# Two sums of weights of a seven-product unit made by accumulating DMAs, one over a tile that ScalarE negates

## The chip, the core and the metric

The kernel runs on one core of a Trainium2 chip. The metric is the time of one execution in microseconds (us); the profile's own span is a little shorter. Engines are named as the profile names them: PE (TensorE's matmuls), PEld (its weight loads), DVE (VectorE), ACT (ScalarE), POOL (GpSimd) and SP (SyncE, which here issues the loads).

## What is computed

A decoder trunk of two layers on 256 positions of width 2048, in float32. The part that the change touches is the second half of a layer, the feed-forward block with a hidden width of 5632:

```python
h = rms_norm(x, ffn_norm[l])
x = x + (jax.nn.silu(h @ w_gate[l]) * (h @ w_up[l])) @ w_down[l]
```

The first half (a projection `w_in`, spatial gating and dilated attention, a projection `w_out`) is not touched.

## The kernel before

All matrix products run in a split form: an operand is cut into a high part, which ACT makes by a copy to a shorter float, and a low part, which DVE makes as operand minus high part. A product is then three matmuls (high by high, high by low, low by high). For weights `split_w` does this: `wh` is the high tile (ACT), `wl` the low tile (DVE), each 128x2048, for a slab of 1 MB that SP has loaded as a tile `raw`.

The feed-forward block goes in units (function `unit`). A unit has to multiply a two by two block matrix of activations by a two by two block matrix of weights, B11, B12, B21 and B22, each a 1 MB quarter. It does so with seven products in place of eight, the Winograd form of Strassen's scheme. The seven run on PE in the order r1, r5, r6, r2, r7, r3, r4, each of 12 matmuls of 512 columns, and add into four PSUM banks named C, CX, CZ and CY. Each has a preparation p1 to p7 that splits its weights:

- `early` makes e = B12 - B11 in a new tile, and over B12's tile B22 - B12, the sum that p7 splits;
- p1 splits B11, and then makes over its tile the sum that p6 splits;
- p5 splits e, p6 splits that sum;
- p2 makes over B11's tile the sum that p4 splits (B21 minus it), and then splits B21;
- p7 splits B12's tile, p3 splits B22, p4 splits B11's tile.

So before the change a unit has four sums of tiles on DVE: e, the one over B12's tile, and two over B11's tile. Behind the seven products stand four plain slabs of weights, 24 matmuls each.

A layer has 17 units: eleven for gate and up (in chunks of four, four and three), and after each chunk two for down. The two down units of a layer's third chunk have quarters of half the size (128x1024). Both layers make 34.

The order of the instructions is written out by the program itself: a list of items (one a product or a plain slab) is run in order; `prep_more` prepares an item as soon as the slots of a ring (UNIT_RING = 6, most items take two) allow it, about three items ahead of PE. `early` is called one item before p1 (`early_at`; five items before for a layer's first unit). Side work (copies out of PSUM, transposes, gating) is put between by `run_jobs`, when a planner's account of the engines' queues (class `Queues`, with costs `act_cost` and `dve_cost`) says that its input is ready. Every engine runs its own instructions in that order and waits on semaphores. ACT, DVE and POOL are called through a wrapper, so that their instructions have line L90 in the profile; matmuls have L836 (`mm3`), the loads L796 (`dma_one`), transposes L253.

Of the kernel before, what the change touches and what calls it, by code (L numbers as in the profile page):

```python
# [11 lines left out]
ACTF = mybir.ActivationFunctionType  # L12
ALU = mybir.AluOpType
# [10 lines left out]
W = 512  # L24
# [8 lines left out]
KC = 4  # L33
HK = 2
S_GU = 4
FORMS = ("11", "22", "S1", "S3", "S2", "12", "S4")

SLOTS = 22
PLAIN_RAW, PLAIN_RING = 3, 4
# [102 lines left out]
def trunk_kernel(ctx: ExitStack, tc: tile.TileContext, aps: dict):  # L142
    nc = tc.nc
    PSUM = bass.MemoryType.PSUM
    q = Queues()
    act = Engine(q, nc.scalar, "act", act_cost)
    dve = Engine(q, nc.vector, "dve", dve_cost)
# [16 lines left out]
    def slot(shape, dtype, name):  # L164

        return gen.tile(list(shape), dtype, tag="g", name=name)
# [65 lines left out]
    def drain(ready):  # L232
        stuck = 0
        while not ready():
            assert stuck < 2000, "operand is never made"
            stuck += 1
            q.pe += 100
            run_jobs(1000)
# [344 lines left out]
    class Forms:  # L583
# [5 lines left out]
        def at(self, f):  # L589
            h = self.halves[FORMS.index(f)]  # L590
            return h[:, 0, :self.s, :], h[:, 1, :self.s, :]
# [27 lines left out]
    def make_forms(F, xg):  # L619

        def quarter(t, h):
            return xg[:, h, :F.s, t * P:(t + 1) * P]
        a11, a12, a21, a22 = quarter(0, 0), quarter(0, 1), quarter(1, 0), quarter(1, 1)

        def split(f, src):
            hi, lo = F.at(f)
            act.activation(out=hi, in_=src, func=ACTF.Copy)
            dve.tensor_tensor(out=lo, in0=src, in1=hi.bitcast(F32), op=ALU.subtract)
            F.ready.add(f)
        split("11", a11)  # L630
        split("22", a22)
        dve.tensor_tensor(out=a22, in0=a21, in1=a22, op=ALU.add)
        dve.tensor_tensor(out=a21, in0=a11, in1=a21, op=ALU.subtract)
        yield
        split("S1", a22)
        split("12", a12)
        dve.tensor_tensor(out=a11, in0=a22, in1=a11, op=ALU.subtract)
        dve.tensor_tensor(out=a12, in0=a12, in1=a11, op=ALU.subtract)
        yield
        split("S2", a11)  # L640
        split("S3", a21)
        split("S4", a12)

# [50 lines left out]
    class Chunk:  # L694
# [32 lines left out]
        def form(self, f, k):  # L727
            drain(lambda: self.F is not None)
            return self.F.get(f, k)
# [61 lines left out]
    def dma_one(r):  # L791
        n = sum(src.shape[1] for src in r.srcs)
        r.tile = slot([P, n, W], F32, "raw")
        k = 0
        for src in r.srcs:
            nc.sync.dma_start(out=r.tile[:, k:k + src.shape[1], :], in_=src)  # L796
            k += src.shape[1]
        live[0] += 1
# [6 lines left out]
    def need(r):  # L805
        while r.tile is None:
            dma_one(raws[n_raw[0]])
            n_raw[0] += 1
        return r.tile

    def split_w(src, parts=1):

        n = src.shape[1]
        if 2 * n <= 4:
            both = slot([P, 2, n, W], F32R, "w")
            wh, wl = both[:, 0], both[:, 1]
        else:
            wh, wl = slot([P, n, W], F32R, "wh"), slot([P, n, W], F32R, "wl")
        saved, q.chain = q.chain, q.pe
        for k in range(parts):  # L820
            sl = slice(k * n // parts, (k + 1) * n // parts)
            act.activation(out=wh[:, sl, :], in_=src[:, sl, :], func=ACTF.Copy)
            dve.tensor_tensor(
                out=wl[:, sl, :], in0=src[:, sl, :], in1=wh[:, sl, :].bitcast(F32), op=ALU.subtract)
        q.chain = saved
        return wh, wl

    def w_sum(out, in0, in1, op):
        saved, q.chain = q.chain, q.pe
        dve.tensor_tensor(out=out, in0=in0, in1=in1, op=op)  # L830
        q.chain = saved

    def mm3(out, x, wh, wl, start, stop):
        hi, lo = x
        for n, (a, b) in enumerate(((hi, wh), (hi, wl), (lo, wh))):
            nc.tensor.matmul(  # L836
                out=out, lhsT=a, rhs=b, start=start and n == 0, stop=stop and n == 2,
                skip_group_check=True)
# [32 lines left out]
    def unit(s, quarter, plains, form, done, lead=1):  # L871

        bank = {}
        b11, b12, b22, b21 = (Raw([quarter(*kn)], UNIT_RAW) for kn in ((0, 0), (0, 1), (1, 1), (1, 0)))
        raws.extend((b11, b12, b22, b21))
        U = {}

        def new_bank(name):  # L880
            drain(lambda: mm_lease.free)
            mm_lease.free.pop(0)
            bank[name] = mm_p.tile([P, W], F32, tag="mm", name="C" + name)

        def copy(out, in_):
            saved, q.chain = q.chain, q.pe
            act.activation(out=out, in_=in_, func=ACTF.Copy)
            q.chain = saved

        def early():  # L890
            x11, x12, x22 = need(b11), need(b12), need(b22)
            U["e"] = slot([P, s, W], F32, "e")
            live[0] += 1
            w_sum(U["e"], x12, x11, ALU.subtract)
            w_sum(x12, x22, x12, ALU.subtract)

        def p1(it, parts=1):
            it.w = split_w(b11.tile)
            w_sum(b11.tile, b12.tile, b11.tile, ALU.add)

        def p5(it, parts=1):
            it.w = split_w(U["e"])
            live[0] -= 1

        def p6(it, parts=1):
            it.w = split_w(b11.tile)

        def p2(it, parts=1):
            w_sum(b11.tile, need(b21), b11.tile, ALU.subtract)
            it.w = split_w(b21.tile)  # L910
            live[0] -= 1

        def p7(it, parts=1):
            it.w = split_w(b12.tile)
            live[0] -= 1

        def p3(it, parts=1):
            it.w = split_w(b22.tile)
            live[0] -= 1

        def p4(it, parts=1):
            it.w = split_w(b11.tile)
            live[0] -= 1

        def product(it, f, name, start):
            wh, wl = it.w
            for k in range(s):
                x = form(f, k)
                mm3(bank[name], x, wh[:, k, :], wl[:, k, :], start and k == 0, k == s - 1)
                q.pe += 3 * MM_NS  # L930
                run_jobs()

        def r1(it):
            new_bank("1")
            product(it, "11", "1", True)
            new_bank("X")
            copy(bank["X"], bank["1"])

        def r5(it):
            new_bank("Z")  # L940
            product(it, "S1", "Z", True)
            U["s5"], U["s3"] = (tmp.tile([P, W], F32, tag="u", name=n) for n in ("s5", "s3"))
            copy(U["s5"], bank["Z"])

        def r6(it):
            product(it, "S2", "X", False)
            new_bank("Y")
            copy(bank["Y"], bank["X"])

        def r2(it):  # L950
            product(it, "12", "1", False)

        def r7(it):
            product(it, "S3", "X", False)
            copy(U["s3"], bank["X"])

        def r3(it):
            product(it, "S4", "Y", False)
            w_sum(bank["Z"], bank["Z"], U["s3"], ALU.add)

        def r4(it):
            product(it, "22", "X", False)
            w_sum(bank["Y"], bank["Y"], U["s5"], ALU.add)

        for p, r in ((p1, r1), (p5, r5), (p6, r6), (p2, r2), (p7, r7), (p3, r3), (p4, r4)):
            items.append(Item(1 if s <= 2 else 2, UNIT_RING, p, r))
        early_at[len(items) - 7 - lead] = early

        names = {(0, 0): "1", (1, 0): "Y", (0, 1): "X", (1, 1): "Z"}
        for i, (n, srcs, ops) in enumerate(plains):  # L970
            r = Raw(srcs, UNIT_RAW)
            raws.append(r)

            def prep(it, parts=1, r=r):
                it.w = split_w(need(r))
                live[0] -= 1

            def run(it, i=i, n=n, ops=ops):
                wh, wl = it.w
                for t in range(NT):  # L980
                    for k, op in enumerate(ops):
                        mm3(bank[names[n, t]], op(t), wh[:, k, :], wl[:, k, :], False, k == len(ops) - 1)
                        q.pe += 3 * MM_NS
                        run_jobs()
                    if i >= len(plains) - 2:
                        add(done(n, t, bank[names[n, t]]), FFN_LIMIT)
            items.append(Item(2, UNIT_RING, prep, run))
# [238 lines left out]
```

## Time and profile before

| what | before |
|---|---|
| median of 3 runs | 2301.93 us (2301.18 to 2302.52) |
| profiled execution | 2301.2 us |
| its span | 2299.0 us |
| PE busy | 2261.3 us (98%) |
| DVE busy | 1834.0 us (80%) |
| ACT busy | 1325.0 us (58%) |
| POOL busy | 52.4 us (2%) |
| DMA queue of SP | 438.69 MB, 53.0% of 16 engines' span |

The span is the time between the first and the last profiled instruction; the profiled execution's own time is 2.2 us more. A busy share is that of the engine's instructions, and matmuls overlap, so that 98% of PE doesn't say that no matmul waited. DMAs issued by POOL don't occur in this kernel.

### The profile page before, as it was taken

The page shows a single profiled execution, that of the slowest core. Times are in us where ns is not written, and L with a number is a line of the kernel's source. Part 1 is how long each engine was busy: PE and PEld are TensorE (multiplying, and loading weights), DVE is VectorE, ACT ScalarE, POOL GpSimd, SP SyncE. Part 2 cuts the span into 40 slices and gives each one's busy share as a digit, 9 for nine tenths or more (in the row PEclk, how much of TensorE's full clock was granted, in tenths as well). Part 3 has the DMA queues.
Part 4 walks back from the last instruction along what each step waited for, and adds up shares of the span by engine and source line. Part 5 has one row for each costly group of instructions (what it writes and reads, how often), then busy time and mean ns, then how long its engine had stood idle before and what let it go on. Part 6 is the DMA issues. An engine that isn't in the chain of part 4 may idle for free.

```text
span 2299.0 us, 25930 instructions
## 1 busy us (share of the span) xinstructions
PE 2261.3 (98%) x10249; PEld 1864.1 (81%) x10249; DVE 1834.0 (80%) x1721; ACT 1325.0 (58%) x1590; POOL 52.4 (2%) x36
## 2 busy tenths in 40 slices
PE   9999999999999999999999999999999999999999
PEld 7888888878788878888788888887787888788887
DVE  6666766889999898998765666768899998989986
ACT  6455565565664665656555555646656556556563
POOL 0100000000000000000000001000000000000000
PEclk9999999999999999999999999999999999999999
DMA  9554455454465644745545444554545556447453
GB/s 361 176 183 165 165 175 204 174 198 165 183 237 183 224 179 159 264 181 201 183 174 193 164 165 165 183 212 173 183 165 198 223 186 235 165 165 274 165 201 110
DMA packets 66937, 440.33 MB, mean 192 GB/s; under 512 B 8064, under 2 KB 8576, under 8 KB 16768
## 3 DMA queue, kind: packets, MB, share of 16 engines
q1 hardware_dynamic: 66816, 438.69, 53.0%
q8 instruction: 80, 1.31, 0.2%
q14 instruction: 41, 0.34, 0.0%
HBM read 436.56 MB, written 2.10 MB: 191 GB/s over the span
## 4 chain that ended last, share of the span: by engine, by line
PE 77%; DVE 13%; issue 5%; ACT 3%; DMA 2%; SPq 0%; DVEq 0%; ACTq 0%
PE Z L836 30%; PE CX L836 15%; PE C L836 12%; PE CY L836 9%; PE CZ L836 8%; DVE wl L90 6%; ACT wh L90 2%; DVE raw L90 1%; PE sc L462 1%; DVE w L90 1%; DVE e L90 1%; PE hTp L253 1%; DMA gn<-in_k_norm 1%; PE qkp L253 1%; DVE hF L90 1%
## 5 line engine op out<-in xcount | busy, mean ns | idle before, releaser
L90 DVE TENSOR_TENSOR wl<-raw,wh 128x2048 fp32r<-128x2048 f32 x316 | 717.3, 2287 | 139.3 <-ACT wh L90 136.5
L90 ACT ACTIVATE wh<-raw 128x2048 fp32r<-128x2048 f32 x316 | 597.0, 1912 | 165.3 <-PE CX L836 56.3
L836 PE MATMUL Z<-w,xT 128*128 128x512 f32 x2688 | 641.5, 395 | 1.8 <-DVE xT L90 1.0
L836 PEld LDWEIGHTS Z<-w,xT 128*128 128x128 f32 x2688 | 499.2, 188 | 106.2 <-DVE w L90 1.6
L90 DVE TENSOR_TENSOR w<-raw,w 128x1024 fp32r<-128x1024 f32 (+1 forms) x313 | 376.9, 1217 | 214.8 <-ACT w L90 209.7
L90 ACT ACTIVATE w<-raw 128x1024 fp32r<-128x1024 f32 (+1 forms) x313 | 315.5, 1049 | 28.2 <-DMA raw<-in_w_in 9.1
L90 DVE TENSOR_TENSOR raw<-raw 128x2048 f32<-128x2048 f32 (+1 forms) x102 | 220.7, 2164 | 2.5
L836 PE MATMUL CX<-wh,fF 128*128 128x512 f32 x528 | 175.5, 391 | 1.5 <-ACT s L90 1.5
L836 PE MATMUL C<-wh,fF 128*128 128x512 f32 x352 | 118.7, 393 | 0.0
L836 PEld LDWEIGHTS CX<-wh,fF 128*128 128x128 f32 x528 | 99.1, 188 | 23.5 <-ACT s L90 2.4
L836 PE MATMUL CY<-wh,fT 128*128 128x512 f32 x352 | 115.9, 390 | 0.4
L836 PE MATMUL C<-wh,fT 128*128 128x512 f32 x352 | 115.6, 389 | 0.0
L836 PE MATMUL CZ<-wh,fT 128*128 128x512 f32 x352 | 115.5, 389 | 0.0
L836 PE MATMUL CX<-wh,fT 128*128 128x512 f32 x352 | 115.5, 389 | 0.0
L836 PE MATMUL CX<-wl,fF 128*128 128x512 f32 x264 | 102.7, 389 | 0.0
L90 ACT ACTIVATE CX<-C 128x512 f32<-128x512 f32 x34 | 19.8, 582 | 125.0 <-PE C L836 125.0
L836 PE MATMUL Z<-w,bT 128*128 128x512 f32 x384 | 89.9, 391 | 0.0
L836 PE MATMUL Z<-w,aT 128*128 128x512 f32 x384 | 89.1, 390 | 0.0
L836 PEld LDWEIGHTS Z<-w,aT 128*128 128x128 f32 x384 | 71.8, 188 | 14.8
L836 PEld LDWEIGHTS Z<-w,bT 128*128 128x128 f32 x384 | 71.8, 188 | 14.7
L836 PE MATMUL CY<-wh,fF 128*128 128x512 f32 x240 | 78.9, 390 | 0.0
L836 PEld LDWEIGHTS CY<-wh,fT 128*128 128x128 f32 x352 | 66.1, 188 | 15.6 <-issue 2.0
(191 smaller groups left out, 3445.0 us busy)
## 6 DMA issues: line engine op xcount, KB each, us to landing
raw<-in_w_in SPq DMA_DIRECT2D x109, 1024.0 KB, 4.8
raw<-in_w_gate SPq DMA_DIRECT2D x88, 1024.0 KB, 4.8
raw<-in_w_up SPq DMA_DIRECT2D x88, 1024.0 KB, 4.9
raw<-in_w_down SPq DMA_DIRECT2D x72, 1024.0 KB, 4.9
raw<-in_w_out SPq DMA_DIRECT2D x32, 1024.0 KB, 4.8
raw<-in_w_down SPq DMA_DIRECT2D x32, 512.0 KB, 4.6
raw<-in_w_in SPq DMA_DIRECT2D x5, 512.0 KB, 8.1
xstage<-in_xT SPq DMA_DIRECT2D x8, 256.0 KB, 7.4
```

The costliest lines, as they stand in the source:

```text
L90: return f(**kw)
L253: nc.tensor.transpose(out=tp[:, i, t * P:(t + 1) * P], in_=src_of(t)[:, (c0 + i) * P:(c0 + i + 1) * P], identity=ident)
L462: nc.tensor.matmul(out=sc[:, g, :n], lhsT=L.kv[pair, g][:, h, t * P:(t + 1) * P], rhs=kT[:, h, :n], start=True, stop=True)
L836: nc.tensor.matmul(out=out, lhsT=a, rhs=b, start=start and n == 0, stop=stop and n == 2, skip_group_check=True)
```

## The change

The sum over B12's tile is no longer made on DVE. ACT negates the tile in place (a copy with scale -1), and a DMA issued by POOL then adds B22 to it, read a second time from DRAM. The sum that p4 splits is made in the same way: as soon as p6 has split B11's tile, a DMA issued by POOL adds B21 to it from DRAM; p2 then only splits B21. For the signs to fit, the sum that p6 splits is now made as e - B22, the negative of what it was, and so the form of the activations in that product is the negative of S2 (`make_forms`: a11 - a22 in place of a22 - a11, and an addition in place of a subtraction behind it). The activations' work keeps its count of instructions. Each accumulating DMA is cut into pieces by `max_dma_last_dim=2 * W`.

```diff
         def early():
             x11, x12, x22 = need(b11), need(b12), need(b22)
             U["e"] = slot([P, s, W], F32, "e")
             live[0] += 1
             w_sum(U["e"], x12, x11, ALU.subtract)
-            w_sum(x12, x22, x12, ALU.subtract)
+            saved, q.chain = q.chain, q.pe
+            act.activation(out=x12, in_=x12, func=ACTF.Copy, scale=-1.0)
+            q.chain = saved
+            nc.gpsimd.dma_start(
+                out=x12, in_=quarter(1, 1), accum_op=ALU.add, max_dma_last_dim=2 * W)
 
         def p1(it, parts=1):
             it.w = split_w(b11.tile)
-            w_sum(b11.tile, b12.tile, b11.tile, ALU.add)
+            w_sum(b11.tile, U["e"], b22.tile, ALU.subtract)
...
         def p6(it, parts=1):
             it.w = split_w(b11.tile)
+            nc.gpsimd.dma_start(
+                out=b11.tile, in_=quarter(1, 0), accum_op=ALU.add, max_dma_last_dim=2 * W)
 
         def p2(it, parts=1):
-            w_sum(b11.tile, need(b21), b11.tile, ALU.subtract)
-            it.w = split_w(b21.tile)
+            it.w = split_w(need(b21))
             live[0] -= 1
...
         def r6(it):
-            product(it, "S2", "X", False)
+            product(it, "-S2", "X", False)
```

The planner counts the new costs, so side work moves as well. The place shown is the second down unit of a layer's first chunk. On DVE before, from e to p2's split (`raw_4748` is B11's tile, `raw_4778` B12's, `raw_4799` B22's, `raw_4818` B21's; `xs` are additions to the residual):

```order
L90 TENSOR_TENSOR e_4850<-raw_4778,raw_4748 128x2048
L90 TENSOR_TENSOR raw_4778<-raw_4799,raw_4778 128x2048
L90 TENSOR_TENSOR wl_4878<-raw_4748,wh_4877 128x2048
L90 TENSOR_TENSOR raw_4748<-raw_4778,raw_4748 128x2048
L90 TENSOR_TENSOR xs0_85<-C1_4667,xs0_85 128x512
L90 TENSOR_TENSOR wl_4908<-e_4850,wh_4907 128x2048
L90 TENSOR_TENSOR xs1_86<-CX_4681,xs1_86 128x512
L90 TENSOR_TENSOR xs0_85<-CY_4724,xs0_85 128x512
L90 TENSOR_TENSOR wl_4940<-raw_4748,wh_4939 128x2048
L90 TENSOR_TENSOR xs1_86<-CZ_4690,xs1_86 128x512
L90 TENSOR_TENSOR raw_4748<-raw_4818,raw_4748 128x2048
L90 TENSOR_TENSOR wl_4961<-raw_4818,wh_4960 128x2048
```

The same stretch of DVE now (`raw_4764` is B11's tile, `raw_4785` B12's, `raw_4804` B22's, `raw_4825` B21's):

```order
L90 TENSOR_TENSOR e_4855<-raw_4785,raw_4764 128x2048
L90 TENSOR_TENSOR wl_4884<-raw_4764,wh_4883 128x2048
L90 TENSOR_TENSOR raw_4764<-e_4855,raw_4804 128x2048
L90 TENSOR_TENSOR xs0_85<-C1_4673,xs0_85 128x512
L90 TENSOR_TENSOR wl_4914<-e_4855,wh_4913 128x2048
L90 TENSOR_TENSOR xs1_86<-CX_4687,xs1_86 128x512
L90 TENSOR_TENSOR xs0_85<-CY_4729,xs0_85 128x512
L90 TENSOR_TENSOR wl_4946<-raw_4764,wh_4945 128x2048
L90 TENSOR_TENSOR xs1_86<-CZ_4695,xs1_86 128x512
L90 TENSOR_TENSOR wl_4967<-raw_4825,wh_4966 128x2048
```

Two sums are gone, the one behind e and the one ahead of p2's split; the rest stands as it stood. On ACT before, in the same unit, from the split of the last plain slab ahead of the unit to p4's split:

```order
L90 ACTIVATE wh_4846<-raw_4730 128x2048
L90 ACTIVATE wh_4877<-raw_4748 128x2048
L90 ACTIVATE wh_4907<-e_4850 128x2048
L90 ACTIVATE wh_4939<-raw_4748 128x2048
L90 ACTIVATE CX_4957<-C1_4943 128x512
L90 ACTIVATE wh_4960<-raw_4818 128x2048
L90 ACTIVATE s5_4979<-CZ_4966 128x512
L90 ACTIVATE wh_4982<-raw_4778 128x2048
L90 ACTIVATE CY_5000<-CX_4957 128x512
L90 ACTIVATE wh_5002<-raw_4799 128x2048
L90 ACTIVATE wh_5020<-raw_4748 128x2048
```

And on ACT now:

```order
L90 ACTIVATE wh_4851<-raw_4735 128x2048
L90 ACTIVATE raw_4785<-raw_4785 128x2048
L90 ACTIVATE wh_4883<-raw_4764 128x2048
L90 ACTIVATE wh_4913<-e_4855 128x2048
L90 ACTIVATE wh_4945<-raw_4764 128x2048
L90 ACTIVATE CX_4964<-C1_4950 128x512
L90 ACTIVATE wh_4966<-raw_4825 128x2048
L90 ACTIVATE s5_4985<-CZ_4972 128x512
L90 ACTIVATE wh_4988<-raw_4785 128x2048
L90 ACTIVATE CY_5006<-CX_4964 128x512
L90 ACTIVATE wh_5008<-raw_4804 128x2048
L90 ACTIVATE wh_5026<-raw_4764 128x2048
```

The negation stands ahead of p1's split, which it was not behind before; the last row, p4's split of B11's tile, now waits for a DMA of POOL where it waited for DVE. POOL has no instruction in this unit before, and now the two DMAs.

## Rows read from the trace of the kernel before

**Rows 1.** The page's first part: busy time, share, instructions of each engine.

```profile
PE 2261.3 (98%) x10249; PEld 1864.1 (81%) x10249; DVE 1834.0 (80%) x1721; ACT 1325.0 (58%) x1590; POOL 52.4 (2%) x36
```

**Rows 2.** Busy time by stretch: first layer's feed-forward block, then second layer's first half.

```profile
core 0: us, PE busy (x) PEld busy (x) DVE busy (x) ACT busy (x) POOL busy (x), PEclk, DMA share, GB/s
400.00:1130.00 730.00, 712.76 (x3182) 585.31 (x3180) 643.18 (x416) 431.22 (x372) 0.69 (x1) 1.00 0.54 195
1130.00:1560.00 430.00, 429.75 (x2017) 358.51 (x2018) 281.15 (x452) 241.27 (x441) 24.88 (x14) 1.00 0.51 181
```

**Rows 3.** Waits of PE: who waited for whom, total us, times, longest us.

```profile
PE C L836 <- DVE wl L90: 12.7, 14, 1.2
PE CZ L836 <- DVE s L90: 5.4, 4, 1.4
```

**Rows 4.** Groups by shape: DVE's sums over a tile, ACT's split (busy us, mean ns).

```profile
L90 DVE TENSOR_TENSOR raw<-raw 128x2048 f32<-128x2048 f32 x90 | 206.0, 2289 | 2.1
L90 DVE TENSOR_TENSOR raw<-raw 128x1024 f32<-128x1024 f32 x12 | 14.7, 1225 | 0.4
L90 ACT ACTIVATE wh<-raw 128x2048 fp32r<-128x2048 f32 x316 | 597.0, 1912 | 165.3 <-PE CX L836 56.3 <-DVE wl L90 52.4 <-PE CZ L836 25.0
```

**Rows 5.** Timeline of the unit shown in order: DVE, ACT, PE (start us, us).

```profile
648.11 2.29 DVE L90 TENSOR_TENSOR wl<-raw,wh 128x2048 fp32r<-128x2048 f32 x1 [1.34 <-ACT wh L90]
650.44 2.29 DVE L90 TENSOR_TENSOR e<-raw 128x2048 f32<-128x2048 f32 x1
652.77 2.29 DVE L90 TENSOR_TENSOR raw<-raw 128x2048 f32<-128x2048 f32 x1
654.98 2.28 DVE L90 TENSOR_TENSOR wl<-raw,wh 128x2048 fp32r<-128x2048 f32 x1
...
660.11 2.28 DVE L90 TENSOR_TENSOR wl<-e,wh 128x2048 fp32r<-128x2048 f32 x1
...
664.38 2.29 DVE L90 TENSOR_TENSOR wl<-raw,wh 128x2048 fp32r<-128x2048 f32 x1 [0.79 <-ACT wh L90]
...
667.19 2.28 DVE L90 TENSOR_TENSOR raw<-raw 128x2048 f32<-128x2048 f32 x1
669.39 6.88 DVE L90 TENSOR_TENSOR wl<-raw,wh 128x2048 fp32r<-128x2048 f32 x3
...
662.42 1.92 ACT L90 ACTIVATE wh<-raw 128x2048 fp32r<-128x2048 f32 x1 [3.64 <-DVE wl L90]
...
668.42 1.91 ACT L90 ACTIVATE wh<-raw 128x2048 fp32r<-128x2048 f32 x1
...
674.56 1.92 ACT L90 ACTIVATE wh<-raw 128x2048 fp32r<-128x2048 f32 x1 [0.93 <-PE C L836]
...
671.73 0.50 PE L836 MATMUL C<-wl,hF 128*128 128x512 f32 x1 [0.90 <-DVE wl L90]
...
680.02 0.39 PE L836 MATMUL CX<-wl,hF 128*128 128x512 f32 x1
```

**Rows 6.** Timeline of PE in the chunk's last gate unit: the two matmuls that waited.

```profile
579.03 0.47 PE L836 MATMUL CZ<-wh,fF 128*128 128x512 f32 x1 [1.35 <-DVE s L90]
...
586.20 0.50 PE L836 MATMUL C<-wl,fF 128*128 128x512 f32 x1 [1.24 <-DVE wl L90]
```

**Rows 7.** Timeline of an ordinary gate unit: p6's low part (DVE), first matmuls of r4 (PE).

```profile
530.85 2.28 DVE L90 TENSOR_TENSOR wl<-raw,wh 128x2048 fp32r<-128x2048 f32 x1
...
550.18 0.39 PE L836 MATMUL CX<-wl,fF 128*128 128x512 f32 x1
```

**Rows 8.** Loads between 600 and 690 us: GB/s in 40 slices; tile raw's landings.

```profile
GB/s 269 197 0 7 0 0 29 350 87 0 135 331 69 335 291 401 382 379 131 350 55 328 84 0 0 0 0 0 266 200 95 393 339 200 422 393 411 441 426 149
...
DMA to landing us min/median/max: 4.7/4.9/8.0
```

**Rows 9.** Groups on POOL: its smallest frequent operations.

```profile
L90 POOL TENSOR_TENSOR qf<-rsq,mhalf 128x8 f32<-128x8 f32 x16 | 35.6, 2227 | 375.9 <-DVE rsq L90 375.9
L90 POOL TENSOR_TENSOR r<-rsq,mhalf 128x2 f32<-128x2 f32 x4 | 2.8, 698 | 925.3 <-DVE rsq L90 925.3
```

More of the change, by code (lines that the diff above doesn't have):

```diff
@@ L35 @@
 S_GU = 4
-FORMS = ("11", "22", "S1", "S3", "S2", "12", "S4")
+FORMS = ("11", "22", "S1", "S3", "-S2", "12", "S4")
 SLOTS = 22
@@ L636, in make_forms @@
         split("12", a12)
-        dve.tensor_tensor(out=a11, in0=a22, in1=a11, op=ALU.subtract)
-        dve.tensor_tensor(out=a12, in0=a12, in1=a11, op=ALU.subtract)
+        dve.tensor_tensor(out=a11, in0=a11, in1=a22, op=ALU.subtract)
+        dve.tensor_tensor(out=a12, in0=a12, in1=a11, op=ALU.add)
         yield
-        split("S2", a11)
+        split("-S2", a11)
         split("S3", a21)
```

## Prediction

> **What bounds the kernel now.** The page's first part comes first: PE is busy for 98% of the span [rows 1], so a saving on any other engine is worth only the waits of PE that it ends. The table by stretch tells where such waits can be. In the second layer's first half PE stands still for 430.00 - 429.75 = 0.25 us, in the first layer's feed-forward block for 730.00 - 712.76 = 17 us, with DVE busy for 643.18 of 730 us there [rows 2]. The units of the change lie in that block. The table of waits names the releasers: PE waited 14 times for DVE's low parts of weights in bank C, 12.7 us in all, and 4 times for DVE's reading of a bank that CZ needs, 5.4 us [rows 3]. What DVE's lateness costs is mostly in these 18.1 us; two such blocks of 17 us idle, 34 us or 1.5%, are the most that any change to DVE can give back, whatever it saves in DVE's own time.
>
> **What is removed.** Two sums a unit go from DVE, 30 units with full quarters and 4 with halves: 60 x 2.289 + 8 x 1.225 = 147 us of DVE work [rows 4]. Nearly all of it lay beside PE's work. What it is worth must be read where PE waits.
>
> The unit shown in order is the second down unit of a chunk [rows 5]. PE waits 0.90 us in r2 for the low part of B21, which p2's split makes. In front of that split DVE makes the sum for p4, and in front of all the sum for p7. The rest of the sum is what stands in their place. Its e starts when it did, since DVE waited for ACT just ahead of it (1.34 us, at 648.11), so nothing backs up into this unit.
>
> **What is added on ACT.** A negation of 34 tiles, taken at the price of a split of the same size, 1.91 us [rows 4]. It must wait for e, which reads the tile, and p1's split is queued behind it on ACT. In the unit: e ends at 652.73, the negation at 654.6, p1's high part at 656.6; DVE's p1 low part starts at 656.6 where it started at 654.98 [rows 5]. So one of the two sums taken from DVE is spent on waiting for ACT, and what follows is 1.6 us later than before, not 2.3 us earlier: p6's low part runs from 666.0 to 668.3 instead of 664.38 to 666.67. (p6's high part started when the low part of e was done, 662.4 [rows 5], and moves along.) The second sum is saved in full: p2's low part starts where the sum at 667.19 stood, plus 1.6, and ends at 668.8 + 2.3 = 671.1, against 669.39 + 2.29 = 671.7 before. **The wait of r2 shrinks by 0.6 us**, of 0.90.
>
> For the sum over all units: eight such down units at 0.6 give 4.8 us. The four last gate units of a chunk wait twice, 1.35 and 1.24 us [rows 6]; the second hangs on p2's low part behind a sum with a DVE that works without a break, and I take it as gone (5.0 us). The first hangs on a DVE queue that the negation holds up as well, and I take two thirds of 5.4, 3.6 us. The two waits of the 14 that are left give 1 us at most. Together 14 us. The ordinary gate units wait for nothing of DVE in these rows and give nothing. Forms of activations: the same count of instructions, no change.
>
> **What is added on POOL and the DMA engines.** Two transfers of 1 MB a unit, 60 MB and 4 more in halves. POOL is nearly empty in the block (0.69 us of 730 [rows 2]), so neither transfer queues there. Who waits for them is ACT, and behind a waiting ACT its copies out of PSUM and the next splits.
>
> The sum for p7 has time: ready for the DMA at 654.6, it is split at 668.42 [rows 5], 13.8 us later. The sum for p4 has not. Its DMA can start when p6's low part has been made, at 668.3 by the working above. r4 wants p4's low part at its second matmul, at 680.02 [rows 5], less the 0.6 gained, so 679.4. In front of that lie ACT's 1.92 and DVE's 2.29 us. So the tile must have landed by 679.4 - 4.2 = 675.2: **an allowance of 6.9 us**, in which p4's split can also slip from 674.56 without any cost. In an ordinary gate unit the same working gives much more: p6's low part ends at 533.1, r4's second matmul is at 550.18, less 4.2 that is 12.8 us [rows 7]. The tight units are the eight down units and, by the same crowded DVE queue, the four last gate units: twelve.
>
> How long does an accumulating DMA take? No row shows one. The nearest is a plain load of 1 MB issued by SP: 4.7 us when nothing else runs, up to 8.0 beside another one [rows 8]. The engines move up to 441 GB/s [rows 8], so 2.4 us of the 4.7 is movement. The low end is the plain load, 4.7 us. An accumulation has to read the tile that it writes, a second pass of up to 2.4 us. About half of the time another load is under way, and I add half of the 3.3 us that this costs at most, 1.6. For POOL's part in starting it, the nearest rows are its tiny operations, 0.7 to 2.2 us [rows 9]; I take the lower. That is 4.7 + 2.4 + 1.6 + 0.7 = **9.4 us**. The high end takes all of the 3.3 and the 2.2: 12.6 us.
>
> The Trainium skill, "DMA: Bandwidth & Descriptors" (Anatomy of one DMA, the GpSimd path), gives a DMA from POOL as 2.0 us plus its bytes at 436 GB/s, an estimate of 4.4 us for this tile; by that page alone nothing would be late and the sum would be 2287. "Collectives: The Full Stack" (The bandwidth ceiling) says that an add in the DMA engines reads two sources and halves the rate, which speaks against the change and would make it 6.8, by a hair in time. No run so far shows either.
>
> **The sum.** 9.4 us against an allowance of 6.9 makes r4 wait 2.5 us in twelve units: 30 us. Less the 14 us gained, +16. The profiled execution took 2301.2 us (2.2 over its span, 0.7 under the median), so **2317 us**. At the high end the wait is 5.7 x 12 = 68 us, less 14, and the time 2355; at the low end there is no wait and it is 2287, with all 18.1 us of waits gone 2283. The traffic itself, 64 MB over 438, some of it in two passes, fits: the queue is busy for about half of the block [rows 2], and loads have several us in hand.
>
> **Rivals.**
> In time: the accumulation lands in under 7.5 us, because the second read runs beside the write and loads don't collide. Then only the gain is left: 2301.2 - 14 = 2287, between 2282 and 2296. For it: the DMA engines are idle for 46% of the block [rows 2]; against it: bursts of loads in the very stretch in which it runs [rows 8]. It decides at about 8.1 us (1.2 us x 12 = 14).
>
> A draw: about 8.1 us, gain and waits cancel, 2301 +- 4.
>
> Much later: the transfer takes 15 us, because POOL writes its many small pieces (order shows the tile as eight pieces of 256 a partition) slowly. Then twelve units wait 8.1 us, the 18 ordinary gate units 2.2: 97 + 40 - 14 = +123, 2424. The place is the same, r4; it starts to be felt in gate units at 12.8 us.
>
> The change not doing what it says, a sum still on DVE, is excluded by the order of the instructions.
>
> **How the numbers follow.** Late in the tight units only: 0.50. Much later: 0.06. In time: 0.30. Draw: 0.14. A measurement of this kernel tells 0.2% (4.6 us) from no change; so faster 0.30, same 0.14, slower 0.56. The likeliest case gives 2317. The range has to reach into the case in time to leave out no more than 2 in 10, and up to the high end of the transfer: 2285 to 2355. Its own range, for the case slower alone, is 2306 to 2355.
>
> **What would show it.** Right: r2 in the down units waits less, no DVE sum ahead of p2's split, p6's low part later by 1.6 us; ACT's split for p4 held by a DMA, PE waiting in CX at r4 in the down units, and nothing there in ordinary gate units. Wrong: the accumulations land 7 us after p6's low part, and PE's idle time in the block falls from 17 us to about 10; or ACT waits for a DMA in gate units too. An error in the allowance (p6's low part not later) would move the result by up to 1.6 x 12 = 19 us down.

## The result and the profile after

The changed kernel takes 2662.64 us (median of 4 runs, 2658.69 to 2666.06) against 2302.22 before (4 runs; the 2301.93 above is from three of them): 1.156 times as long, 95% interval 1.154 to 1.159. The direction was forecast, the size was not: 2317 was predicted, with a range that ended at 2355, and the loss is 360 us in place of 15.

The page of the changed kernel begins as follows (busy time of each engine; granted clock of PE in 40 slices; DMA queues with packets, MB and share of 16 engines).

```profile
span 2657.0 us, 26239 instructions
PE 2344.0 (88%) x10249; PEld 1915.0 (72%) x10249; DVE 1698.1 (64%) x1653; ACT 1378.6 (52%) x1624; POOL 155.6 (6%) x104
PEclk9999999998889988899999999999988899888999
q1 hardware_dynamic: 66816, 438.69, 45.5%
q0 software_dynamic: 66624, 67.11, 16.1%
```

Beside [rows 1], DVE is busy for 136 us less (147 were taken from it, and its other work came to 11 us more), and PE's share fell from 98 to 88%. Span minus PE's busy time is PE's idle time: 313.0 us, against 37.7 before. But PE's busy time grew as well, by 82.7 us for the same 10249 matmuls, and the granted clock shows lower slices, all in the two feed-forward blocks. Idle and slower matmuls together, 275 + 83, are the whole difference of the spans, 358 us.

Who PE waited for stands in its table of waits, and why that one was late in ACT's (who waited for whom, total us, times, longest us).

```profile
PE CX L836 <- ACT s L90: 245.8, 30, 15.7
PE CX L836 <- DVE wl L90: 25.0, 30, 1.3
```

```profile
ACT wh L90 <- DMA raw<-in_w_gate: 236.8, 21, 17.1
ACT wh L90 <- DMA raw<-in_w_down: 108.1, 8, 19.0
```

The 14 waits in bank C for DVE's low parts [rows 3] no longer stand in the table, as the change meant. In their place PE waits 30 times in CX: 29 times in the 30 full units and once in a unit with halves. The instruction named, ACT's copy s, is only what ACT did last before the wait ended: it stood behind p4's split, and that split waited for the accumulating DMA. The timeline of the last gate unit of the first chunk shows the whole chain (POOL, ACT, PE; start us, us, and in brackets the idle time before with its releaser):

```profile
598.92 1.57 POOL L911 DMA_DIRECT2D raw<-in_w_gate  x1 [13.11 <-DVE wl L90]
...
621.43 1.91 ACT L90 ACTIVATE wh<-raw 128x2048 fp32r<-128x2048 f32 x1 [16.79 <-DMA raw<-in_w_gate]
623.25 0.58 ACT L90 ACTIVATE s<-CX 128x512 f32<-128x512 f32 x1
...
623.88 0.80 PE L836 MATMUL CX<-wh,fF 128*128 128x512 f32 x1 [12.62 <-ACT s L90]
625.72 0.79 PE L836 MATMUL CX<-wl,fF 128*128 128x512 f32 x1 [1.05 <-DVE wl L90]
626.31 1.05 PE L836 MATMUL CX<-wh,fF 128*128 128x512 f32 x2
627.16 0.63 PE L836 MATMUL CX<-wl,fF 128*128 128x512 f32 x1
...
630.29 0.62 PE L836 MATMUL C<-wh,fT 128*128 128x512 f32 x2
630.75 0.39 PE L836 MATMUL C<-wl,fT 128*128 128x512 f32 x1
```

The DMA was issued at 598.92 and landed 22.4 us later. The rows of PE show the second part of the loss too. After the wait of 12.62 us two matmuls take 0.85 us from start to start (626.31 to 627.16), 0.43 us each; 4 us later two take 0.46 (630.29 to 630.75), 0.23 each, as is usual. The granted clock is 0.50 from 623.88 to 628.87, the lower of its two levels (1.2 GHz for 2.4), and 1.00 from 629.83 to 631.66. Slower matmuls stand behind each of the 30 longest waits in CX of this trace, so these waits are paid a second time.

How long the transfers took is in the DMA issues (tile, queue, count, KB, median us from issue to landing). The rows of POOL are, in order, the fifth product's sum in gate units, the seventh's there, and both in the full down units.

```profile
raw<-in_w_gate SPq DMA_DIRECT2D x88, 1024.0 KB, 6.9
raw<-in_w_up POOLq DMA_DIRECT2D x22, 1024.0 KB, 11.6
raw<-in_w_gate POOLq DMA_DIRECT2D x22, 1024.0 KB, 20.2
raw<-in_w_down POOLq DMA_DIRECT2D x16, 1024.0 KB, 13.3
```

The seventh's sum took 20.2 us where 9.4 was predicted; even plain loads went from 4.9 [rows 8] to 6.9. And here is what the DMA engines did in seven microseconds in the middle of that landing (606 to 613 us; queue, packets, MB, share of 16 engines):

```profile
q1 hardware_dynamic: 299, 2.20, 78.2%
q0 software_dynamic: 330, 0.34, 29.8%
```

Nearly the same number of packets went from either queue, 330 and 299, but a packet of q1 (SP's loads) has up to 8 KB and one of q0 (the accumulations, cut by `max_dma_last_dim`) 1 KB. So the accumulation got 0.34 of 2.54 MB, 49 GB/s. That suggested the theory for the experiments: **the two queues take turns packet by packet, so small pieces beside large ones starve.** The Trainium skill, "DMA: Bandwidth & Descriptors" (Queues, rings and completion order), states it as a rule: an engine goes round between its queues at packet granularity. The counts agree, and a shorter stretch in which both queues are always busy (613.8 to 615.4 us) shows the turn itself:

```profile
q1 hardware_dynamic: 64, 0.52, 81.0%
q0 software_dynamic: 64, 0.07, 25.2%
```

64 packets of either queue in 1.6 us on 16 engines are one of each for an engine in 0.4 us, and the first 0.4 us alone (613.8 to 614.2) have 16 of each. By the Trainium skill a packet there holds some 9 to 17 descriptors; a turn here is one packet as the profile counts them, 1 KB or 8 KB, and so the accumulation got an eighth of the loads' bytes.

Rivals were: small pieces are slow by themselves, whatever runs beside them; the fifth's sum or the negation is to blame; the added traffic as such.

### The profile page after: what moved, and what is told of

Read it like the earlier page. It is cut to its first block, busy times and chain, and to the rows that moved or that the text cites. A ratio compares the mean times of both kernels' runs of the same rounds, so it can differ in the third digit from the quotient of the medians.

```text
span 2657.0 us, 26239 instructions
## 1 busy us (share of the span) xinstructions
PE 2344.0 (88%) x10249; PEld 1915.0 (72%) x10249; DVE 1698.1 (64%) x1653; ACT 1378.6 (52%) x1624; POOL 155.6 (6%) x104
## 3 DMA queue, kind: packets, MB, share of 16 engines
q0 software_dynamic: 66624, 67.11, 16.1%
## 4 chain that ended last, share of the span: by engine, by line
PE 55%; issue 24%; DMA 16%; DVE 2%; ACT 2%; POOL 1%; SPq 0%; POOLq 0%; ACTq 0%; DVEq 0%
PE Z L836 29%; PE CX L836 9%; DMA raw<-in_w_gate 7%; DMA raw<-in_w_down 7%; PE C L836 6%; PE CZ L836 5%; PE CY L836 4%; DVE wl L90 2%; ACT wh L90 1%; PE sc L462 1%; DMA gn<-in_k_norm 1%; PE qkp L253 1%; POOL raw L898 1%; PE o L494 0%; DMA raw<-in_w_in 0%
## 5 line engine op out<-in xcount | busy, mean ns | idle before, releaser
L836 PE MATMUL CX<-wh,fF 128*128 128x512 f32 x528 | 206.1, 455 | 161.7 <-ACT s L90 161.7
L836 PEld LDWEIGHTS CX<-wh,fF 128*128 128x128 f32 x528 | 118.7, 225 | 196.0 <-ACT s L90 170.7
L90 ACT ACTIVATE raw<-raw 128x2048 f32<-128x2048 f32 (+1 forms) x34 | 61.8, 1816 | 199.5 <-DVE e L90 179.9
L836 PE MATMUL CX<-wh,hF 128*128 128x512 f32 x192 | 77.4, 469 | 80.2 <-ACT s L90 80.2
L836 PE MATMUL CX<-wl,fF 128*128 128x512 f32 x264 | 122.8, 465 | 18.2 <-DVE wl L90 18.2
L836 PEld LDWEIGHTS CX<-wh,hF 128*128 128x128 f32 x192 | 44.2, 230 | 93.0 <-ACT s L90 83.6
L836 PEld LDWEIGHTS CX<-wl,fF 128*128 128x128 f32 x264 | 58.6, 222 | 40.9 <-DVE wl L90 28.3
L898 POOL DMA_DIRECT2D raw<-in_w_up x22 | 34.1, 1548 | 832.8 <-ACT raw L90 832.8
## 6 DMA issues: line engine op xcount, KB each, us to landing
raw<-in_w_up POOLq DMA_DIRECT2D x22, 1024.0 KB, 11.6
raw<-in_w_gate POOLq DMA_DIRECT2D x22, 1024.0 KB, 20.2
raw<-in_w_down POOLq DMA_DIRECT2D x16, 1024.0 KB, 13.3
```

The lines of the kernel that those rows point to most:

```text
L90: return f(**kw)
L836: nc.tensor.matmul(out=out, lhsT=a, rhs=b, start=start and n == 0, stop=stop and n == 2, skip_group_check=True)
L898: nc.gpsimd.dma_start(out=x12, in_=quarter(1, 1), accum_op=ALU.add, max_dma_last_dim=2 * W)
```

## The experiments

The first four take the change apart. Times are medians with the interval of the ratio to the kernel before (2301.92 in the runs of this group).

**pieces_8k**: both DMAs in pieces of 8 KB, like the loads.

```diff
-                out=x12, in_=quarter(1, 1), accum_op=ALU.add, max_dma_last_dim=2 * W)
+                out=x12, in_=quarter(1, 1), accum_op=ALU.add, max_dma_last_dim=16 * W)
...
-                out=b11.tile, in_=quarter(1, 0), accum_op=ALU.add, max_dma_last_dim=2 * W)
+                out=b11.tile, in_=quarter(1, 0), accum_op=ALU.add, max_dma_last_dim=16 * W)
```

> Only change against the changed kernel: the accumulating DMAs are cut into pieces of 8 KB (a whole row of a partition) in place of 1 KB. Theory (the DMA engines take turns by packet, so a 1 KB accumulating packet of about 102 ns goes through for every 8 KB load packet of about 309 ns, and the transfer is starved while loads run): the sum for the seventh product lands 9 to 13 us after its issue in place of 14 to 25, PE's waits in CX fall from 8 us a unit to 0 to 4, and the time is 2300 to 2350 us. Rival (the accumulation itself, or POOL's start of it, is what takes so long, whatever the size of a piece): landing stays near 20 us and the time near 2660.

Measured: 2369.23 us, ratio 1.029 (1.028 to 1.031). Four fifths of the loss, 293 us, hang on the size of the pieces. The same bytes are added; the seventh's sum lands in 11.0 us and PE's great wait shrinks to a tenth (page of this kernel, its issues, its waits of PE):

```profile
q1 hardware_dynamic: 66816, 438.69, 49.9%
q0 software_dynamic: 9792, 67.11, 15.1%
...
raw<-in_w_gate POOLq DMA_DIRECT2D x22, 1024.0 KB, 11.0
...
PE CX L836 <- ACT s L90: 24.4, 12, 3.9
```

The time is a little above the range expected; the rest, 67 us, has other causes.

**fifth_only**: the fifth product's sum as in the change, the seventh's back on DVE (with the changed signs an addition).

```diff
         def p6(it, parts=1):
             it.w = split_w(b11.tile)
-            nc.gpsimd.dma_start(
-                out=b11.tile, in_=quarter(1, 0), accum_op=ALU.add, max_dma_last_dim=2 * W)
...
         def p2(it, parts=1):
-            it.w = split_w(need(b21))
+            w_sum(b11.tile, need(b21), b11.tile, ALU.add)
+            it.w = split_w(b21.tile)
```

> Only the sum for the fifth product (over B12's tile) is made by negation and accumulating DMA, in pieces of 1 KB; the one for the seventh is again a sum on VectorE. Theory (what costs the time is the wait of the seventh product's split for a tile that lands too late; the fifth's has 13.8 us and lands in 8.6 to 13): no wait of PE in CX for a copy behind it, 2285 to 2310 us. Rival (the added traffic slows every load, and these the splits): 2350 us or more, with waits for plain loads.

Measured: 2314.25, ratio 1.005 (1.003 to 1.007), above what was expected. With 1 KB pieces too the fifth's sum lands in 10.0 us, in time for its split, and nobody waits for it. But instead of a gain there is a loss of 12 us (the four runs go from 2308 to 2318).

**seventh_only**: the reverse, with no negation; the fifth's sum on DVE.

```diff
-            saved, q.chain = q.chain, q.pe
-            act.activation(out=x12, in_=x12, func=ACTF.Copy, scale=-1.0)
-            q.chain = saved
-            nc.gpsimd.dma_start(
-                out=x12, in_=quarter(1, 1), accum_op=ALU.add, max_dma_last_dim=2 * W)
+            w_sum(x12, x22, x12, ALU.subtract)
```

> Only the sum for the seventh product is made by an accumulating DMA, in pieces of 1 KB; the one for the fifth is made on VectorE, with no negation on ScalarE. Theory: nearly the whole loss is here, 2600 to 2660 us, with the split of the seventh product waiting 10 to 20 us for its DMA. Rival (the two transfers of a unit hold each other up, or the negation on ScalarE is what delays): under 2450 us.

Measured: 2638.91, ratio 1.146 (1.144 to 1.149). Half the added traffic, one of two edits, and 337 of the 360 us. The added traffic as such is out, since fifth_only adds the same 33.56 MB for 12 us: it is the seventh's sum.

```profile
PE CX L836 <- ACT s L90: 240.6, 31, 17.0
...
raw<-in_w_gate POOLq DMA_DIRECT2D x22, 1024.0 KB, 19.6
```

**negation_alone**: the signs and the negation of the change, but both sums made by DVE as additions; no accumulating DMA.

```diff
             act.activation(out=x12, in_=x12, func=ACTF.Copy, scale=-1.0)
             q.chain = saved
-            nc.gpsimd.dma_start(
-                out=x12, in_=quarter(1, 1), accum_op=ALU.add, max_dma_last_dim=2 * W)
+            w_sum(x12, x22, x12, ALU.add)
```

(and p6 and p2 as in fifth_only)

> No accumulating DMA: ScalarE negates B12's tile and VectorE adds B22 to it; the sum for the seventh product is on VectorE too. So only the order of work on ScalarE is that of the change. By the working of the prediction the negation makes what follows it on VectorE later by about 4 us in the tight units (1.6 with the sum gone, the sum of 2.3 back): 2310 to 2345 us. Rival (ScalarE's idle time hides it): 2298 to 2306 us.

Measured: 2329.65, ratio 1.012 (1.011 to 1.014): the negation at this place costs 28 us. So the fifth's DMA itself is a gain, from 2329.65 to 2314.25. Where the 28 us come from is read in the waits of DVE and of PE, and in the last gate unit of the second chunk (ACT, DVE, PE):

```profile
DVE raw L90 <- ACT raw L90: 64.0, 34, 2.0
...
PE CZ L836 <- DVE s L90: 13.1, 4, 3.3
...
829.22 1.92 ACT L90 ACTIVATE raw<-raw 128x2048 f32<-128x2048 f32 x1 [8.08 <-DVE e L90]
...
826.90 2.28 DVE L90 TENSOR_TENSOR e<-raw 128x2048 f32<-128x2048 f32 x1
831.16 2.29 DVE L90 TENSOR_TENSOR raw<-raw 128x2048 f32<-128x2048 f32 x1 [1.98 <-ACT raw L90]
...
844.44 0.74 DVE L90 SCALAR_TENSOR_TENSOR s<-CY,r,s 128x512 f32<-128x512 f32 x1
...
845.33 0.77 PE L836 MATMUL CZ<-wh,fF 128*128 128x512 f32 x1 [3.29 <-DVE s L90]
```

The same unit in the kernel before (DVE, PE):

```profile
816.60 2.29 DVE L90 TENSOR_TENSOR e<-raw 128x2048 f32<-128x2048 f32 x1
...
832.21 0.74 DVE L90 SCALAR_TENSOR_TENSOR s<-CY,r,s 128x512 f32<-128x512 f32 x1
...
833.10 0.47 PE L836 MATMUL CZ<-wh,fF 128*128 128x512 f32 x1 [1.35 <-DVE s L90]
```

ACT is there early and stands still for 8.08 us until e is ready; then the negation takes its 1.9 us, and DVE, which adds B22 to the negated tile next, waits 1.98 us for it. From e to the gating work s DVE now takes 17.54 us where it took 15.61, and r5, which can't have its bank CZ before s is done, waits 3.29 us where it waited 1.35: the delay of 1.93 us is DVE's wait for the negation. The four waits for s grew from 5.4 [rows 3] to 13.1 us. That is 7.7 of the 19 us by which PE's idle time grew; the largest other part is 5.5 us in CZ, for DVE's additions to the residual. PE's busy time grew by 12. In fifth_only the sum behind the negation is gone from DVE, but in the same unit DVE waits 2.50 us for a copy that stands behind the negation on ACT, and s comes 15.86 us after e: nothing is won.

The next four test the theory of turns, and whether the negation must cost anything (kernel before here: 2301.63).

**loads_1k**: the change as it is, with the *loads* cut to 1 KB. It separates "small pieces are slow" from "small pieces beside large ones are slow".

```diff
-            nc.sync.dma_start(out=r.tile[:, k:k + src.shape[1], :], in_=src)
+            nc.sync.dma_start(out=r.tile[:, k:k + src.shape[1], :], in_=src, max_dma_last_dim=2 * W)
```

> The change whole, with both accumulating DMAs in 1 KB pieces as before, but the plain loads of weights that SP issues in dma_one cut to 1 KB pieces too. Theory (the two queues take turns packet by packet, so an accumulation of 1 KB packets gets one eighth of the bytes beside loads of 8 KB packets): now both queues move the same bytes in a turn, so the seventh product's sum lands in 10 to 14 us where it took 20 and PE's wait in CX for ACT falls from 246 us to under 90; the loads themselves land later than 8 us. Time 2330 to 2440, open at the top because loads of 1 KB may be slow in themselves. Rival (small accumulating pieces are slow whatever runs beside them, for POOL's writing of them or their second read): landing stays at 17 us or more, the wait at 200 us or more, time 2630 or above.

Measured: 2447.01, ratio 1.064 (1.062 to 1.065). Nothing of the accumulations was touched, and the seventh's sum lands in 13.5 us for 20.2, the wait in CX falls from 246 to 63 us and the time by 216 us (7 us more than the range; the loads themselves now take 8.4). This is the experiment that settles it. The page, the issues and the waits of PE:

```profile
q1 hardware_dynamic: 427648, 438.69, 56.7%
q0 software_dynamic: 66624, 67.11, 17.5%
...
raw<-in_w_gate SPq DMA_DIRECT2D x88, 1024.0 KB, 8.4
...
raw<-in_w_gate POOLq DMA_DIRECT2D x22, 1024.0 KB, 13.5
...
PE CX L836 <- ACT s L90: 62.7, 23, 6.0
```

In seven microseconds inside such a landing (1822 to 1829 us) equal turns are now equal bytes:

```profile
q0 software_dynamic: 790, 0.81, 71.8%
q1 hardware_dynamic: 876, 0.88, 43.1%
```

**pieces_4k**: as pieces_8k with `8 * W`, 4 KB.

> The change with both accumulating DMAs in pieces of 4 KB, between the 1 KB of the change (20.2 us median landing of the seventh's sum in gate units) and the 8 KB already run (11.0 us). Theory of turns by packet: 16 packets to an engine for a half-tile share of 64 KB, each turn an accumulating packet of some 0.32 us and a load's of 0.31 us, 10 us and some 2 to 3 for start and end: 12 to 14 us, PE's wait in CX for ACT 30 to 80 us, time 2375 to 2440. Rival (a threshold between 1 KB and 8 KB, or a cost for each piece in POOL): landing within 1 us of one of the two ends.

Measured: 2437.5, ratio 1.059 (1.057 to 1.061); landing 13.7 us, wait 63.9 us, all inside the theory's ranges. The queues' rows are

```profile
q1 hardware_dynamic: 66816, 438.69, 49.2%
q0 software_dynamic: 17472, 67.11, 14.9%
```

and with these rows the landings can be worked out. A queue's share times 16 engines times the span, over its packets, is the time of a packet: in the change 103 ns for q0 and 290 ns for q1, so a turn of 393 ns moves 1007 bytes of the accumulation on each engine, and 1.05 MB would need 25.6 us if loads ran beside it throughout. By the same working 8.3 us in pieces_8k, 10.6 in pieces_4k and 10.1 in loads_1k. The 393 ns agree with the turn of 0.4 us counted above. The landings measured there, 11.0, 13.7 and 13.5, are each some 3 us more. In the change loads run beside it for only a part of the time, and 20.2 is the median of 8.7 to 25.2.

**seventh_8k**: as seventh_only with `16 * W`.

> Only the seventh product's sum by DMA, in 8 KB pieces, with no negation and the fifth's sum on DVE. If what is left of the loss in pieces_8k (67 us) is the negation's 28 us plus the wait for this sum, this run shows about 2310 to 2345, with waits of PE in CX for ACT of 15 to 35 us in the last gate units and down units. Rival (with the negation gone the sum has time, and two thirds of a DVE sum a unit is a gain): 2285 to 2300, faster than before.

Measured: 2351.0, ratio 1.022 (1.020 to 1.023), 6 us above the range and far from the rival. Even in 8 KB pieces, without any negation, the seventh's sum costs 49 us net, because it still lands in 11.2 us. PE's idle time grew by 29 us (2348.0 - 2280.9 against 37.7) and its busy time by 20.

```profile
PE CX L836 <- ACT s L90: 21.9, 14, 3.5
```

**fifth_negated_first**: only the fifth's sum by DMA, but ScalarE negates B12's tile *ahead* of e. Then e is made as B11 - B12, and the activations' S1 is stored negated.

```diff
-            w_sum(U["e"], x12, x11, ALU.subtract)
-            w_sum(x12, x22, x12, ALU.subtract)
+            saved, q.chain = q.chain, q.pe
+            act.activation(out=x12, in_=x12, func=ACTF.Copy, scale=-1.0)
+            q.chain = saved
+            w_sum(U["e"], x12, x11, ALU.add)
+            nc.gpsimd.dma_start(
+                out=x12, in_=quarter(1, 1), accum_op=ALU.add, max_dma_last_dim=2 * W)
...
-            w_sum(b11.tile, b12.tile, b11.tile, ALU.add)
+            w_sum(b11.tile, U["e"], b22.tile, ALU.add)
...
+            if f == "-S1":
+                act.activation(out=hi, in_=src, func=ACTF.Copy, scale=-1.0)
+                dve.scalar_tensor_tensor(
+                    out=lo, in0=src, scalar=-1.0, in1=hi.bitcast(F32),
+                    op0=ALU.mult, op1=ALU.subtract)
```

> Only the fifth product's sum by DMA in 1 KB pieces, but the tile of B12 is negated by ScalarE ahead of e instead of behind it: e is made with the other sign and S1 is kept negated, so that the negation can run as soon as the tile has landed and p1's split does not queue behind a wait for e. Theory (the 28 us of the negation are its wait for e on ACT with p1's split behind it): ACT no longer waits for e, DVE has one sum a unit less, and the time falls from 2314 to between 2285 and 2303. Rival (the cost is ACT's 1.9 us a unit wherever it stands, because e and p1 then wait for ACT instead): 2305 to 2325.

Measured: 2286.99 (2286.71 to 2287.54), ratio 0.994 (0.992 to 0.995). **This kernel beats both**, the one before by 14.6 us. ACT waits for nothing in front of the negation (groups by shape; the last number is the idle time before it), the fifth's sum lands in time with 11.8 us, and PE has less idle time than in any other kernel here, 24.9 us:

```profile
L90 ACT ACTIVATE raw<-raw 128x2048 f32<-128x2048 f32 x30 | 57.2, 1906 | 0.0
...
PE C L843 <- DVE wl L90: 5.5, 8, 1.0
...
raw<-in_w_up POOLq DMA_DIRECT2D x22, 1024.0 KB, 11.8
```

The last two part the gain and add up the costs (kernel before: 2301.88).

**negated_first_no_dma**: the same with the fifth's sum on DVE.

```diff
-            nc.gpsimd.dma_start(
-                out=x12, in_=quarter(1, 1), accum_op=ALU.add, max_dma_last_dim=2 * W)
+            w_sum(x12, x22, x12, ALU.add)
```

> The kernel fifth_negated_first with the fifth product's sum made by VectorE as an add and no accumulating DMA: as many DVE sums as before, ScalarE's negation ahead of e. It parts what fifth_negated_first gained (14.6 us) into the DMA's share and the rest. Theory (the gain is the sum of 2.3 us a unit that DVE no longer makes, and the negation ahead of e is free): 2297 to 2308, about as before. Rival (the new order of e behind a negation is a gain in itself, and the DMA adds little): 2284 to 2292.

Measured: 2301.65, ratio 1.000 (0.999 to 1.001). A negation ahead of e is free, and the fifth's DMA alone is the gain.

**both_8k_negated_first**: both sums by DMA in 8 KB pieces, negation first.

```diff
+            dve.scalar_tensor_tensor(
+                out=b11.tile, in0=U["e"], scalar=-1.0, in1=b22.tile,
+                op0=ALU.mult, op1=ALU.subtract)
...
             it.w = split_w(b11.tile)
+            nc.gpsimd.dma_start(
+                out=b11.tile, in_=quarter(1, 0), accum_op=ALU.add, max_dma_last_dim=16 * W)
```

> Both sums by accumulating DMAs, in 8 KB pieces, with the negation ahead of e (e with the other sign; p1's tile is made negated in the same DVE instruction). If the costs found so far add up, this is the 2369 of pieces_8k less the 27 us that the place of the negation cost: 2335 to 2350, with PE's wait in CX for ACT still 20 to 30 us, since only the seventh's landing of 11 us makes it. Rival (the seventh's sum was late only because p1 and p6 were late behind the negation): the wait goes under 8 us and the time under 2305.

Measured: 2333.3, ratio 1.014 (1.012 to 1.015), 2 us below the range, with 13.4 us of waiting in CX for ACT's s: less than expected, but far from the rival. The costs nearly add up: the negation's place is worth 27.3 us with the fifth's DMA (2314.25 to 2286.99), 28.0 without it (2329.65 to 2301.65) and 35.9 here (2369.23 to 2333.3); the seventh's sum in 8 KB pieces costs 49 us alone and 46 on top of the best kernel (whose fifth sum stays in 1 KB pieces).

All kernels in one table; idle is the span less PE's busy time, both from the profiled execution (which for fifth_only was 6 us faster than the median, for loads_1k 6 us slower).

| kernel | median us | seventh's landing in gate units, us | PE idle us | PE busy us |
|---|---|---|---|---|
| before | 2302 | (DVE) | 37.7 | 2261.3 |
| the change | 2662.6 | 20.2 | 313.0 | 2344.0 |
| seventh_only | 2638.9 | 19.6 | 291.1 | 2342.8 |
| loads_1k | 2447.0 | 13.5 | 128.7 | 2323.0 |
| pieces_4k | 2437.5 | 13.7 | 124.9 | 2310.8 |
| pieces_8k | 2369.2 | 11.0 | 77.0 | 2288.0 |
| seventh_8k | 2351.0 | 11.2 | 67.1 | 2280.9 |
| both_8k_negated_first | 2333.3 | 11.6 | 56.5 | 2276.7 |
| negation_alone | 2329.7 | (DVE) | 56.7 | 2273.5 |
| fifth_only | 2314.3 | (DVE) | 45.3 | 2261.2 |
| negated_first_no_dma | 2301.7 | (DVE) | 39.2 | 2260.6 |
| fifth_negated_first | 2287.0 | (DVE) | 24.9 | 2260.6 |

## Why the prediction was wrong in its size

**The place and the chain were right.** The prediction named the seventh's sum as the one without time, ACT's split of p4 as what is held, and r4 in bank CX as where PE waits; it said that the fifth's sum has time (10 us of the 13.8 allowed, fifth_only). All of that is in the rows. So is its own sign of being wrong, ACT waiting for a DMA in gate units too.

**The step that failed is the term "half of the 3.3 us that this costs at most, 1.6"** in the 9.4 us for the accumulating DMA. The rest of that sum was not bad: 4.7 + 2.4 + 0.7 is 7.8, and an accumulation with little beside it landed in 8.6 to 8.9 us (POOL's instruction was 1.5 us for the 0.7 taken). But the term for company, bounded at 3.3 by two *loads* side by side, measured about 11 us (20.2 less 8.6 to 8.9). Two loads side by side move packets of the same size; the accumulation's were an eighth of a load's and got an eighth of the bytes in a turn. The prediction had both facts at hand, the eight pieces of 256 elements a partition and the bursts of loads at that moment [rows 8], and didn't put them together: the pieces appear only in the rival "much later", as slow work of POOL. POOL's 1.5 us an instruction speaks against that cause, and loads_1k, which has the same pieces, refutes it. The rival's place was right, and its 0.06 was far too little.

**From there the prediction's own sum comes out.** 20.2 against the allowances of 6.9 (12 units) and 12.8 (18 units) is 13.3 x 12 + 7.4 x 18 = 293 us of waiting in CX; the trace has 246 + 25 there. So the second error follows from the first: "nothing there in ordinary gate units" stood on a landing under 12.8. By place the sum is less exact, and its deviations cancel in part: the second down units of a chunk waited 15.1 to 15.7 us, the first ones 4.3 to 5.8, and the first gate units of the later chunks, ordinary ones by the prediction, 11.5 to 12.7.

**A term was missing: the clock.** The 82.7 us by which PE's busy time grew have no place in the prediction. A wait on PE was priced at its length; in the change it cost 1.3 times that (358 / 275), in seventh_8k 1.7 times (49 / 29).

**The gain of 14 us was right in one part and had the wrong sign in another.** The prediction costed the negation in the second down unit of the first chunk, and that unit was read fairly. After the change p1's low part starts 6.07 us after e, where it was 4.54 [rows 5]: 1.5 later for the 1.6 taken. p6's starts after 14.61 (13.94 before), 0.7 later for 1.6; p2's after 17.40 (18.95 before), 1.5 earlier for 0.6. These are its e and the low parts of p1, p6 and p2 on DVE:

```profile
689.74 2.29 DVE L90 TENSOR_TENSOR e<-raw 128x2048 f32<-128x2048 f32 x1
695.81 2.29 DVE L90 TENSOR_TENSOR wl<-raw,wh 128x2048 fp32r<-128x2048 f32 x1 [3.79 <-ACT wh L90]
...
704.35 2.28 DVE L90 TENSOR_TENSOR wl<-raw,wh 128x2048 fp32r<-128x2048 f32 x1
...
707.14 2.29 DVE L90 TENSOR_TENSOR wl<-raw,wh 128x2048 fp32r<-128x2048 f32 x1
```

r2's waits, 12.7 us in bank C, are down to 1.7 in seventh_8k, with no sum ahead of p2's split and 22 us of waits in CX, and to none in the change. But the sentence "I take two thirds of 5.4", a gain from r5's waits in CZ, has the wrong sign: with the negation behind e they became 7.1 us in fifth_only and 13.1 in negation_alone. (The change's own table has 2.9, but there PE is late by its waits in CX, and DVE's lateness can hide behind them.) Waits that the prediction doesn't list grew too, in CZ for DVE's additions to the residual from 2.5 to 5.8 us in fifth_only. In all, the fifth's half of the change lost 12 us; that its DMA alone is worth 15 is near the 14 by luck. What the seventh's sum is worth off DVE, apart from its landing, no run shows.

**The prices from elsewhere.** The prediction set 4.4 us by the Trainium skill's "DMA: Bandwidth & Descriptors" (Anatomy of one DMA, the GpSimd path) beside its own number; the trace has no accumulation of 1 MB in the change below 8.6. What the Trainium skill's "Collectives: The Full Stack" (The bandwidth ceiling) states, that an add reads two sources and halves the rate, agrees with the trace: in pieces_8k the accumulations took 15.1% x 16 x 2365 us for 67.11 MB, 85 us of an engine for each MB, the loads of the same piece size 43.

What stays open: how the 28 us of the negation divide between waits and slower matmuls unit by unit, and what in a 1 KB piece makes it 103 ns; neither was tried. That the slower matmuls follow from the waits is read from the rows behind each wait and from the table, where busy and idle time rise together; no run separated them.

## What to carry to other kernels

When a transfer is added beside others, compare the size of its packets with theirs, not only its bytes: where the queues take turns by packet, an eighth of the packet size is an eighth of the bandwidth, at the moment when the others are busiest. Cost an inserted instruction on an in-order engine by what stands behind it, on that engine and on the one that needs its result: the negation waited for e, and DVE then waited 2.0 us for it in negation_alone and 2.5 us for a copy behind it in fifth_only, where DVE had been spared a sum of 2.3; ahead of e the same negation was free. Give a sum to the DMA engines only where its user is later than the slowest landing: of two such sums, the one with 13.8 us of time by the prediction's working gained 15 us, and the one with 6.9 lost 49 even in 8 KB pieces, the best form tried.

## What the runs showed of the hardware

- Queues of POOL and SP took turns packet by packet: 330 and 299 packets in 7 us with 1 KB and 8 KB packets, 790 and 876 with 1 KB both; where both were always busy, 64 and 64 in 1.6 us, one of each for each of 16 engines in 0.4 us. A transfer's rate then hangs on the *other* queue's packet size.
- An accumulating DMA cost twice a plain load's engine time for each byte (85 and 43 us per MB at 8 KB); cutting it to 1 KB raised that to 102 us (16.1% x 16 x 2657 us / 67.11 MB), only a fifth more. Small pieces were not slow in themselves.
- In the change a 1 MB accumulation of 1 KB pieces landed in 8.6 to 8.9 us with little beside it and in up to 25.2 us beside loads.
- Behind long waits of PE stood matmuls at half the usual pace: 0.85 us for two behind the wait of 12.62 us, at a granted clock of 0.50, and 0.46 for two 4 us later, at 1.00.
